# The opening of a transformer block by token halves, and another order of a tile's products

## The chip, the cores and the metric

The kernel runs on one core of a Trainium2 chip. The metric is the device time of one execution in microseconds (us), the smaller the better. The engines have these names in the rows: PE is TensorE (matrix products), PEld its weight loads, DVE is VectorE, ACT is ScalarE, POOL is GpSimd, and SP is the engine that issues most of the transfers from memory (rows of its queue say SPq).

## What is computed

One block for 512 tokens of width 1024 in float32: two token mixers (stick-breaking attention and retention) fed from one wide projection, gates, an output projection, a gated feed-forward layer of width 2816, and norms that are modulated by a condition `c`. The change touches the head of it, the first norm with its modulation, and the first eighth of the projection:

```python
c_act = jax.nn.silu(c)
mod = jnp.einsum('bd,de->be', c_act, w_ada[l]) + b_ada[l]
shift1, scale1, gate1, shift2, scale2, gate2 = jnp.split(mod, N_MOD, axis=-1)
hmix = modulate(rmsnorm(x, g_norm1[l]), shift1, scale1)
proj = jnp.einsum('bsd,de->bse', hmix, w_in[l])
sb_q, sb_k, sb_v, r_q, r_k, r_v, r_g, br = jnp.split(proj, IN_SPLITS, axis=-1)
```

`rmsnorm` divides a token by the root of the mean of its squares over the 1024 features and multiplies by a gain; `modulate(h, shift, scale)` is `h * (1 + scale) + shift`.

## The kernel before

**Layout.** Activations lie with the features on the 128 partitions and the 512 tokens along the free axis. The input x is thus eight tiles `xts[0]` to `xts[7]` (tag `o`) of 128 x 512. `HALVES` are the token columns 0 to 255 and 256 to 511.

**Precision by parts.** A product of float32 precision is made of three faster ones: a tensor is split into a high part (`hi`, made by ScalarE as a rounded copy) and a low part (`lo`, the difference, made by VectorE), and hi x hi, hi x lo and lo x hi are added up in PSUM. Only tile 0 of the opening is multiplied unsplit, as plain float32.

**Loads.** All transfers of the opening go out on SP's queue, in the order of the program text: the small vectors `sm`, the eight tiles of x, a piece of the constants `con`, and then for tile after tile two blocks `sraw` of the modulation matrix (`ada_load`) and one block `raw` of `w_in` (`start_weight`; 256 columns of queries, 256 of keys and 512 of values of the first retention head). A buffer that is still in use makes SP wait, and all that is behind it in its queue. For `raw` there are three buffers, and the low part of the weights, `w_lo`, is one of the instructions that free them.

**Up to the first product.** `ccol` is silu(c). Eight products broadcast it over the partitions (`cb`), and two copies bring it to `cact`. Filler products (`keep_busy`) follow. The squares of the x tiles are made by ScalarE (tile 3 by VectorE); VectorE adds up five of them, and TensorE sums the columns by products with ones, four for each half of the tokens (`ssq`). `dot(n, half)` is a modulation column as a VectorE product with a running sum, `dot_pe(0)` the same by TensorE for the shift of tile 0. `rsqrt_rows` turns a half's sums into `r1` in two ScalarE and three VectorE instructions (lines 327 to 331). `mod_gain` and `mod_shift` (ScalarE, lines 415 and 410) add biases to the columns. `h_t` (VectorE, line 431) multiplies x by gain and `r1`; for tile 0 an addition of the shift follows (ScalarE, line 500).

**The loop over eight tiles** (`kt`, lines 514 to 561) issues the loads of tile kt + 2, the dots of tile kt + 1, the low activations `h_lo` of tile kt (VectorE, line 440), the products of tile kt, then for tile kt + 1 `mod_shift`, `mod_gain`, `w_lo` (VectorE, line 425), `h_t` and the high activations `h_hi` (ScalarE, line 437), and `w_hi` of tile kt + 2 (ScalarE, line 421). Products are 4 of queries and keys (`qk_products`) and 4 of values (`v_products`) for each pair of parts, 24 in all, into eight PSUM banks.

**What sets the order.** TensorE, VectorE and ScalarE run the opening in the order of the program text (`manual_schedule`), each engine strictly through its own queue. Behind the opening a scheduler chooses the order.

Of the kernel before, what the change touches and what calls it, by code (L numbers as in the profile page):

```python
# [11 lines left out]
F32 = mybir.dt.float32  # L12
# [7 lines left out]
P = 128  # L20
# [95 lines left out]
def kernel(  # L116
# [60 lines left out]
    xts = []  # L177
    for j in range(KT):
        xt = otile()
        nc.sync.dma_start(xt, xT[j * P : (j + 1) * P, :])  # L180
        xts.append(xt)
# [4 lines left out]
    nc.sync.dma_start(con[:, P:], consts[:, P:NCON])  # L186
# [198 lines left out]
    for kt in range(2):  # L385
        raws[kt] = ada_load(kt)
        wts[kt] = start_weight(kt)
# [56 lines left out]
    with tc.manual_schedule(engines={nc.vector.engine, nc.scalar.engine, nc.tensor.engine}):  # L444

        nc.scalar.preload_act_table_set("natural_log_exp_and_others")
        c = sm[:, SM_C : SM_C + KT]
# [12 lines left out]
        busy = ps()  # L460

        def keep_busy(n, busy=busy):


            for _ in range(n):
                mm(busy, negones, negones[:, 0:1].to_broadcast([P, S]), True, True)

        keep_busy(8)

        sq = {}  # L470
        for j in range(KT):
            sq[j] = tmp()
            if j == 3:
                nc.vector.tensor_mul(sq[j], xts[j], xts[j])
            else:
                nc.scalar.activation(sq[j], xts[j], AF.Square)
            if j == 4:
                nc.vector.tensor_copy(cact[:, 0:S], cb[0])
            elif j == 6:
                nc.scalar.activation(cact[:, S:], cb[1], AF.Copy)  # L480
            if 0 < j < 5:
                nc.vector.tensor_add(sq[0], sq[0], sq[j])
        ssq = []
        for hv in HALVES:
            o = psz()[:, 0:256]
            for j in (5, 0, 6, 7):
                mm(o, ones, sq[j][:, hv], j == 5, j == 7)
            ssq.append(o)
# [10 lines left out]
        for hv in HALVES:  # L499
            nc.scalar.activation(ts[0][:, hv], ts[0][:, hv], AF.Identity, bias=mods[0, 0])  # L500
        hs.append(pair("h"))
        w_hi(1)
        qk_ps = [ps() for _ in range(3)] + [psa()]
# [10 lines left out]
        for kt in range(KT):  # L514
# [45 lines left out]
            if nx + 1 < KT:  # L560
                w_hi(nx + 1)
# [1264 lines left out]
```

## Time and profile before

| | us |
|---|---|
| three timed executions | 1117.97, 1121.2, 1122.1 |
| their median | 1121.2 |
| the profiled execution | 1119.87 |
| its span, from the first to the last instruction | 1118.2 |
| TensorE busy in it | 1102.5 |
| VectorE busy | 872.0 |
| ScalarE busy | 560.8 |
| first product of tile 0 starts | 16.06 |
| first product of tile 1 starts | 22.62 |

A row of the timeline gives the start and the length in us, the engine, the line, the operation, the tiles it writes and reads, how many instructions are merged in the row, and in brackets how long the engine was idle before it and what ended that. A row of the chain of waits gives a start, a length and what the end of the program, followed back, was held up by. Matrix products overlap in the records, so the spacing of their starts is their price, not their length; a plain float32 product shows as two records. A row of the windows gives a stretch, the busy time of PE, PEld, DVE, ACT and POOL with the number of instructions, then the granted clock, the share of the DMA engines and GB/s. A row of the DMA list gives the transfer, its count, the size of each and the median time from issue to landing.

### The profile page before, as it was taken

The numbers are of one execution on the slowest core, as the hardware profiler recorded it, in microseconds if no ns is written. First come the engines' busy times: TensorE is split into PE (matmuls) and PEld (weight loads), VectorE is DVE, ScalarE is ACT, GpSimd is POOL, SyncE is SP. The second block draws the span as 40 slices with busy tenths as digits, with TensorE's granted clock in tenths as the row PEclk, the third lists the DMA queues.
The fourth block names the chain that finished last, engine by engine and source line by source line (L and its number), as shares of the span: only waits on it lengthen the run. The fifth ranks groups of instructions, "written<-read, shape, count | busy, mean of one in ns | idle before, by whom it ended". The sixth has DMA issues, their size and how long they took to land.

```text
span 1118.2 us, 15055 instructions
## 1 busy us (share of the span) xinstructions
PE 1102.5 (99%) x5607; PEld 937.8 (84%) x5607; DVE 872.0 (78%) x1297; ACT 560.8 (50%) x926; POOL 40.4 (4%) x69
## 2 busy tenths in 40 slices
PE   8999999999999999999999999999999999999996
PEld 7888888888888888888888888789988888888886
DVE  7898866847858768487788767767999889888866
ACT  5455445445434645355655653357745544554443
POOL 0000000010020020000000000000000000000000
PEclk9999999999999999999999999999999999999998
DMA  9825551582484285877676459762443544444112
GB/s 360 300 76 194 196 190 61 178 201 73 169 178 162 89 211 192 212 218 207 177 209 166 152 178 309 244 186 58 123 142 114 151 132 132 129 117 131 58 38 76
DMA packets 60553, 181.42 MB, mean 162 GB/s; under 512 B 7488, under 2 KB 9536, under 8 KB 60480
## 3 DMA queue, kind: packets, MB, share of 16 engines
q1 hardware_dynamic: 54464, 166.30, 45.7%
q0 software_dynamic: 5472, 13.63, 7.8%
q8 instruction: 44, 0.72, 0.3%
q10 hardware_dynamic: 544, 0.52, 0.1%
q14 instruction: 29, 0.24, 0.1%
HBM read 148.97 MB, written 16.78 MB: 148 GB/s over the span
## 4 chain that ended last, share of the span: by engine, by line
PE 90%; DVE 4%; DMA 3%; ACT 2%; issue 1%; SPq 0%; DVEq 0%; ACTq 0%
PE ps L230 65%; PE z L230 14%; PE av L230 8%; DMA araw<-wada 1%; PE ps L642 1%; DMA raw<-wp 1%; DVE araw L261 0%; PE z L770 0%; DMA gspill<-g 0%; DVE wlo L210 0%; PE av L642 0%; DMA t<-spill 0%; ACT q L1205 0%; DVE o L1700 0%; DVE h L1515 0%
## 5 line engine op out<-in xcount | busy, mean ns | idle before, releaser
L230 PE MATMUL ps<-h,whi 128*128 128x512 f32 (+1 forms) x1026 | 295.8, 373 | 2.1 <-ACT h L208 1.3
L230 PEld LDWEIGHTS ps<-h,whi 128*128 128x128 f32 x1026 | 186.0, 189 | 35.6 <-ACT h L208 1.7
L208 ACT ACTIVATE whi<-raw 128x1024 fp32r<-128x1024 f32 (+1 forms) x104 | 108.8, 1046 | 184.6 <-PE ps L230 133.8
L230 PE MATMUL ps<-h,wlo 128*128 128x512 f32 (+1 forms) x513 | 188.6, 371 | 0.0
L210 DVE TENSOR_TENSOR wlo<-raw,whi 128x1024 fp32r<-128x1024 f32 (+1 forms) x104 | 124.9, 1201 | 58.5 <-ACT whi L208 57.8
L230 PEld LDWEIGHTS ps<-h,wlo 128*128 128x128 f32 x513 | 97.1, 189 | 16.7
L230 PE MATMUL ps<-s,whi 128*128 128x512 f32 x320 | 98.9, 390 | 0.0
L230 PE MATMUL ps<-q,whi 128*128 128x512 f32 (+1 forms) x368 | 98.5, 385 | 0.0
L859 DVE TENSOR_TENSOR wlo<-s,whi 128x1024 fp32r<-128x1024 f32 x46 | 56.2, 1222 | 43.8 <-ACT whi L855 43.8
L230 PEld LDWEIGHTS ps<-q,whi 128*128 128x128 f32 x368 | 68.0, 188 | 13.3
L855 ACT ACTIVATE whi<-s 128x1024 fp32r<-128x1024 f32 x47 | 49.7, 1057 | 48.0 <-PE ps L230 39.0
L230 PE MATMUL ps<-whi,h 128*128 128x512 f32 x222 | 71.6, 391 | 0.0
L230 PEld LDWEIGHTS ps<-s,whi 128*128 128x128 f32 x320 | 60.1, 188 | 12.7 <-DVE s L210 0.3
L230 PE MATMUL ps<-s,wlo 128*128 128x512 f32 x160 | 62.2, 389 | 0.0
L230 PE MATMUL ps<-q,wlo 128*128 128x256 f32 (+1 forms) x328 | 59.3, 293 | 0.0
L230 PEld LDWEIGHTS ps<-q,wlo 128*128 128x128 f32 x328 | 48.2, 190 | 3.3
L230 PEld LDWEIGHTS ps<-whi,h 128*128 128x128 f32 x222 | 41.7, 188 | 9.6 <-ACT t L1004 0.6
L230 PE MATMUL ps<-wlo,h 128*128 128x512 f32 x111 | 43.2, 390 | 0.0
L632 DVE TENSOR_TENSOR_SCAN s<-s,table 128x1024 f32<-128x1024 f32 x16 | 36.6, 2288 | 6.7 <-ACT s L626 6.7
L230 PE MATMUL ps<-whi,q 128*128 128x512 f32 x128 | 40.7, 389 | 0.0
L230 PE MATMUL z<-q,q 128*128 128x256 f32 (+3 forms) x224 | 40.1, 325 | 0.0
L230 PEld LDWEIGHTS z<-q,q 128*128 128x128 f32 x224 | 34.8, 189 | 3.0 <-DVE q L210 0.2
(352 smaller groups left out, 2185.9 us busy)
## 6 DMA issues: line engine op xcount, KB each, us to landing
raw<-wp SPq DMA_DIRECT2D x136, 512.0 KB, 3.9
araw<-wp SPq DMA_DIRECT2D x30, 512.0 KB, 4.4
s<-wp SPq DMA_DIRECT2D x24, 512.0 KB, 5.9
araw<-wada SPq DMA_DIRECT2D x18, 512.0 KB, 4.7
sraw<-wada SPq DMA_DIRECT2D x16, 512.0 KB, 8.6
q<-qp SPq DMA_DIRECT2D x32, 256.0 KB, 3.9
s<-wada SPq DMA_DIRECT2D x14, 512.0 KB, 6.8
spill<-o POOLq DMA_DIRECT2D x24, 256.0 KB, 4.3
```

Of the source, the lines that this page charges most:

```text
L208: nc.scalar.activation(dst_hi, src, AF.Copy, scale=scale)
L210: return (eng or nc.vector).tensor_sub(dst_lo, src, f(dst_hi))
L230: return nc.tensor.matmul(o, lhs, rhs, start=start, stop=stop, skip_group_check=True).ins
L632: nc.vector.tensor_tensor_scan(n[:, ::-1], n[:, ::-1], d[:, ::-1], 0.0, op0=ALU.mult, op1=ALU.max)
L642: nc.tensor.transpose(at[bank][:, c : c + P], t[:, a + j * P : a + (j + 1) * P], ident)
L855: nc.scalar.activation(hi, t, AF.Copy)
L859: last_low[0] = nc.vector.tensor_sub(lo, t, f(hi))
```

## The change

The loads are halved and reordered, the norm of the first tokens is separated from that of the second, the fillers are moved, and inside the loop two orders are changed.

```diff
-    xts = []
-    for j in range(KT):
-        xt = otile()
-        nc.sync.dma_start(xt, xT[j * P : (j + 1) * P, :])
-        xts.append(xt)
+    xts = [otile() for _ in range(KT)]
+
+    def load_x(js, hv, queue):
+        for j in js:
+            queue.dma_start(xts[j][:, hv], xT[j * P : (j + 1) * P, hv])
...
-    nc.sync.dma_start(con[:, P:], consts[:, P:NCON])
...
-    for kt in range(2):
-        raws[kt] = ada_load(kt)
-        wts[kt] = start_weight(kt)
+    odd = nc.sync
+    for j in range(KT):
+        load_x((j,), slice(0, 256), odd if j % 2 else nc.sync)
+    raws[0] = ada_load(0)
+    first = wpool.tile([P, WCOLS], F32, tag="raw", bufs=BUFS["raw"], name=nm("raw"))
+    load_x(range(8), slice(256, 512), nc.sync)
+    nc.sync.dma_start(first, wp[WIDX["start", 0]])
+    wts[0] = (first, None, None)
+    raws[1] = ada_load(1)
+    wts[1] = start_weight(1)
+    nc.sync.dma_start(con[:, P:], consts[:, P:NCON])
...
+        busy = ps()
...
+        keep_busy(6)
...
-        keep_busy(8)
-
-        sq = {}
+        def square(j, hv, eng):
+            sq = tmp()[:, 0:256]
...
+        r1 = tmp()
+        h0, h1 = HALVES
+        sums = []
         for j in range(KT):
-            sq[j] = tmp()
+            sq = square(j, h0, nc.vector if j % 2 else nc.scalar)
+            if j in (1, 3, 5):
+                nc.vector.tensor_add(sums[-1], sums[-1], sq)
+            else:
+                sums.append(sq)
             if j == 3:
-                nc.vector.tensor_mul(sq[j], xts[j], xts[j])
-            else:
-                nc.scalar.activation(sq[j], xts[j], AF.Square)
...
+                sq = sums.pop()
+                nc.vector.tensor_add(sums[-1], sums[-1], sq)
+        nc.vector.tensor_copy(cact[:, 0:S], cb[0])
+        nc.scalar.activation(cact[:, S:], cb[1], AF.Copy)
+        s0, s1 = (psz()[:, 0:256] for _ in range(2))
+        column_sums(s0, sums, True, True)
         dot(0, 1)
-        r1 = tmp()
+        keep_busy(4)
         dot_pe(0)
-        keep_busy(3)
-        rsqrt_rows(ssq[0], r1[:, HALVES[0]])
+        rsqrt_rows(s0, r1[:, h0])
         mod_gain(0)
-        h_t(0, HALVES[0])
-        rsqrt_rows(ssq[1], r1[:, HALVES[1]])
-        h_t(0, HALVES[1])
+        h_t(0, h0)
+        column_sums(s1, [square(j, h1, nc.scalar) for j in range(3)], True, False)
         mod_shift(0)
-        for hv in HALVES:
-            nc.scalar.activation(ts[0][:, hv], ts[0][:, hv], AF.Identity, bias=mods[0, 0])
+        identity(h0)
+        three, five = (square(j, h1, nc.vector) for j in (3, 5))
+        nc.vector.tensor_add(three, three, five)
+        seven_ = square(7, h1, nc.vector)
+        keep_busy(4)
+        four, six = (square(j, h1, nc.scalar) for j in (4, 6))
+        nc.vector.tensor_add(three, three, four)
+        nc.vector.tensor_add(six, six, seven_)
+        column_sums(s1, [three, six], False, True)
+        rsqrt_rows(s1, r1[:, h1])
+        h_t(0, h1)
+        identity(h1)
...
                 qk_products(hi, ah, ALL)
+                v_products(ah, hi, range(4))
                 qk_products(lo, ah, ALL)
-                if nx + 1 in PE_SHIFT:
-                    dot_pe(nx + 1)
-                v_products(ah, hi, range(4))
                 v_products(ah, lo, range(4))
...
-                w_lo(nx)
                 h_t(nx)
                 h_hi(nx)
+                w_lo(nx)
```

`odd` is SP's queue too, so all sixteen half tiles go out on the one queue, with the two modulation blocks of tile 0 between the eight first and the eight second halves. `column_sums` multiplies each given tile by ones into one bank; `identity` is the addition of the shift to a half of tile 0.

TensorE ahead of the first product before the change (z_165 and z_170 are the column sums of the two halves, ps_134 takes the fillers, ps_178 is the dot on TensorE, and ps_212 is the first bank of products):

```order
L230 MATMUL ps_134<-negones 128x512 x8
L230 MATMUL z_165<-t_158,ones 128x256
L230 MATMUL z_165<-t_143,ones 128x256
L230 MATMUL z_165<-t_160,ones 128x256
L230 MATMUL z_165<-t_163,ones 128x256
L230 MATMUL z_170<-t_158,ones 128x256
L230 MATMUL z_170<-t_143,ones 128x256
L230 MATMUL z_170<-t_160,ones 128x256
L230 MATMUL z_170<-t_163,ones 128x256
L230 MATMUL ps_178<-mod,sraw_102 128x1 x8
L230 MATMUL ps_134<-negones 128x512 x3
L230 MATMUL ps_212<-o_73,raw_104 128x256
```

The same place now, from the last column sum of the first half on (z_170 is the first half's bank, z_171 the second's, ps_241 the first bank of products):

```order
L230 MATMUL z_170<-t_166,ones 128x256
L230 MATMUL ps_125<-negones 128x512 x4
L230 MATMUL ps_182<-mod,sraw_101 128x1 x8
L230 MATMUL z_171<-t_200,ones 128x256
L230 MATMUL z_171<-t_202,ones 128x256
L230 MATMUL z_171<-t_204,ones 128x256
L230 MATMUL ps_125<-negones 128x512 x4
L230 MATMUL z_171<-t_212,ones 128x256
L230 MATMUL z_171<-t_225,ones 128x256
L230 MATMUL ps_241<-o_73,raw_103 128x256
```

The column sums of the second half, five products in place of four, have moved behind the dot and between two groups of fillers; all of them stand ahead of the first product. Six fillers now stand ahead of the broadcast of c.

VectorE from the second half's scaling of tile 0 to the first low activations, before (o_73 is tile 0, o_75 tile 1; L394 is a dot, L425 the low weights, L431 the scaling):

```order
L431 SCALAR_TENSOR_TENSOR o_73<-o_73,sm_196,t_177 128x256
L394 SCALAR_TENSOR_TENSOR sraw_108,sm_228<-sraw_108,cact 128x1024
L394 SCALAR_TENSOR_TENSOR sraw_110,sm_242<-sraw_110,cact 128x1024
L425 TENSOR_TENSOR wlo_115<-raw_112,whi_114 128x1024
L431 SCALAR_TENSOR_TENSOR o_75<-o_75,sm_245,t_177 128x512
L394 SCALAR_TENSOR_TENSOR sraw_220,sm_260<-sraw_220,cact 128x1024
L440 SCALAR_TENSOR_TENSOR h_249<-o_75,shifts,h_249 128x512
```

And now, from the last sums of the second half on (o_73 is tile 0, o_74 tile 1; the lines have moved by 8: L402 is a dot, L433 the low weights, L439 the scaling; L523 and L524 add squares):

```order
L523 TENSOR_TENSOR t_212<-t_212,t_223 128x256
L524 TENSOR_TENSOR t_225<-t_225,t_217 128x256
L329 SCALAR_TENSOR_TENSOR t_231<-t_231 128x256
L330 SCALAR_TENSOR_TENSOR t_231<-z_171,t_231 128x256
L331 SCALAR_TENSOR_TENSOR t_147<-t_231 128x256
L439 SCALAR_TENSOR_TENSOR o_73<-o_73,sm_197,t_147 128x256
L402 SCALAR_TENSOR_TENSOR sraw_113,sm_257<-sraw_113,cact 128x1024
L402 SCALAR_TENSOR_TENSOR sraw_115,sm_271<-sraw_115,cact 128x1024
L439 SCALAR_TENSOR_TENSOR o_74<-o_74,sm_274,t_147 128x512
L433 TENSOR_TENSOR wlo_120<-raw_117,whi_119 128x1024
L402 SCALAR_TENSOR_TENSOR sraw_249,sm_289<-sraw_249,cact 128x1024
L448 SCALAR_TENSOR_TENSOR h_277<-o_74,shifts,h_277 128x512
```

The scaling of tile 1 now follows directly on the second dot, whose result, by way of the gain on ScalarE, it needs; the low weights have moved behind it. The same holds for every later tile.

More of the change, by code (lines that the diff above doesn't have):

```diff
@@ L483, with column_sums @@
-        ssq = []
-        for hv in HALVES:
[L485 to L488, printed above, removed]
+        def square(j, hv, eng):
+            sq = tmp()[:, 0:256]
+            if eng is nc.vector:
+                nc.vector.tensor_mul(sq, xts[j][:, hv], xts[j][:, hv])
+            else:
+                nc.scalar.activation(sq, xts[j][:, hv], AF.Square)
+            return sq
+        def column_sums(o, sums, first, last):
+            for n, sq in enumerate(sums):
+                mm(o, ones, sq, first and n == 0, last and n == len(sums) - 1)
```

17 lines of the change are left out of this document (6 added, 11 removed).

## The prediction

> **What bounds the kernel now.** I read the page first: the shares of busy time and the shares of the chain of waits.
>
> ```profile
> PE 1102.5 (99%) x5607; PEld 937.8 (84%) x5607; DVE 872.0 (78%) x1297; ACT 560.8 (50%) x926; POOL 40.4 (4%) x69
> PE 90%; DVE 4%; DMA 3%; ACT 2%; issue 1%; SPq 0%; DVEq 0%; ACTq 0%
> ```
>
> TensorE is busy for 1102.5 of 1118.2 us. The change neither removes nor adds a product of the real work, so it can only move the point at which TensorE becomes continuously fed. That point lies in the opening, so I read next the chain of waits over the first 70 us (start, length, what).
>
> ```profile
> 9.93 1.84 PE z L230 x8
> 11.80 0.48 ACT t L327
> 14.20 0.48 DVE o L431
> 14.69 0.35 DVE t L329
> 15.50 0.52 ACT o L500
> 16.06 1.56 PE ps L230 x6
> ```
>
> The column sums of the first half end just before 11.80, the logarithm at L327 starts the norm, L431 scales the first half of tile 0 until 14.68, L500 adds the shift until 16.02, and at 16.06 the first real product starts. Everything ahead of 16.06 is what the change rearranges. Behind it the timeline shows who is short (start, length, engine, line, tiles, idle before).
>
> ```profile
> 22.28 1.22 DVE L394 SCALAR_TENSOR_TENSOR sraw<-sraw,cact 128x1024 f32<-128x1024 f32 x1
> 22.62 0.19 PEld L230 LDWEIGHTS ps<-h,whi 128*128 128x128 f32 x1 [0.24 <-ACT shifts L410]
> 23.42 1.22 DVE L425 TENSOR_TENSOR wlo<-raw,whi 128x1024 fp32r<-128x1024 f32 x1
> 23.54 0.39 ACT L415 ACTIVATE sm<-sm,mod,sm 128x1 f32<-128x1 f32 x1 [1.01 <-DVE sraw L394]
> 24.56 0.74 DVE L431 SCALAR_TENSOR_TENSOR o<-o,sm,t 128x512 f32<-128x512 f32 x1
> 25.34 0.72 ACT L437 ACTIVATE h<-o,shifts 128x512 fp32r<-128x512 f32 x1 [1.41 <-DVE o L431]
> 26.37 0.74 DVE L440 SCALAR_TENSOR_TENSOR h<-o,shifts,h 128x512 fp32r<-128x512 f32 x1
> 33.75 0.64 PEld L230 LDWEIGHTS ps<-h,whi 128*128 128x128 f32 x3
> 39.19 0.64 PEld L230 LDWEIGHTS ps<-h,whi 128*128 128x128 f32 x3
> ```
>
> Tile 1's products start at 22.62. A tile of 24 products then lasts 5.44 us (33.75 to 39.19 is one tile), 0.227 a product. VectorE needs for a tile, start to start: 1.14 for a dot (22.28 to 23.42), 1.14 for the low weights (23.42 to 24.56), 0.66 for the scaling L431, 1.15 for the other dot, and for L440 the rest of a period of 4.75 (L440 of tile 1 starts at 21.61, of tile 2 at 26.37). It runs without a gap, so it is 0.69 a tile faster than TensorE. The last place where TensorE waits for that lead is in the first attention scores:
>
> ```profile
> 21.61 0.75 DVE L440 SCALAR_TENSOR_TENSOR h<-o,shifts,h 128x512 fp32r<-128x512 f32 x1
> 50.53 0.69 DVE L552 TENSOR_TENSOR h<-o,h 128x512 fp32r<-128x512 f32 x1
> 55.93 1.06 ACT L208 ACTIVATE whi<-raw 128x1024 fp32r<-128x1024 f32 x1 [4.38 <-PE z L230]
> 57.02 1.23 DVE L210 TENSOR_TENSOR wlo<-raw,whi 128x1024 fp32r<-128x1024 f32 x1 [4.21 <-ACT whi L208]
> 70.75 0.69 DVE L210 TENSOR_TENSOR q<-t,q 128x512 fp32r<-128x512 f32 x1
> 71.49 1.29 PEld L230 LDWEIGHTS z<-q,q 128*128 128x128 f32 x10 [0.24 <-DVE q L210]
> ```
>
> VectorE idles 4.21 us before 57.02 and then has no gap up to the low part q that ends at 71.44; TensorE idles 0.24 for it. At this join whichever of the two is later decides; after it I count a shift as carried to the end.
>
> **The change, part by part.** The sum is made on the profiled execution: 1118.2 us of span, 1119.87 in all. The three timed runs have a median of 1121.2 (1117.97 to 1122.1); with the profiled one the median of four is 1120.5, and that is what I put my shift on.
>
> *Loads.* The prices of the loads and of the early work:
>
> ```profile
> 1.25 3.74 SPq L180 DMA_DIRECT2D o<-xT  x8
> 7.60 1.99 ACT L476 ACTIVATE t<-o 128x512 f32<-128x512 f32 x3 [0.71 <-DMA o<-xT]
> 11.15 1.23 DVE L394 SCALAR_TENSOR_TENSOR sraw<-sraw,cact 128x1024 f32<-128x1024 f32 x1 [1.00 <-DMA sraw<-wada]
> 17.46 1.06 ACT L421 ACTIVATE whi<-raw 128x1024 fp32r<-128x1024 f32 x1 [0.45 <-DMA raw<-wp]
> 9.50:13.30 3.80, 3.80 (x18) 3.17 (x18) 2.39 (x6) 2.26 (x6) 0.00 (x0) 1.00 1.02 407
> o<-xT SPq DMA_DIRECT2D x8, 256.0 KB, 4.3
> raw<-wp SPq DMA_DIRECT2D x136, 512.0 KB, 3.9
> out_dram<-o SPq DMA_DIRECT2D x8, 128.0 KB, 1.8
> ```
>
> SP issues a tile load every 0.47 us. Sixteen halves instead of eight wholes add eight issues, 3.8 us of SP: the last second half goes out near 9.8, the first weight near 10.2 instead of 6.93, the second near 11.6 instead of 8.95. This hides behind the queue, which moves 407 GB/s (last figure of the stretch 9.5 to 13.3), 1.29 us per 512 KB, and is behind anyway: the first modulation half lands at 11.15, so the first weight lands at 13.7 and the second at 17.5 (seen at 17.46). Ahead of the first weight stand the same bytes as before, so 13.7 stays. If the rows of half length moved more slowly, the cover would be gone by what they lose. The first halves are 1 MB; before, 1.25 MB were there at 7.60, so I take 6.9 for the last first half. The nearest transfer of that size, a store at the end of the kernel, lands 1.8 after its issue; from the last issue at 4.5 that gives 6.3, and a store need not price a load, so 6.3 to 7.6.
>
> *TensorE up to the first product.*
>
> ```profile
> 1.10 0.23 DVE L198 TENSOR_SCALAR negones<-ones 128x128 fp32r<-128x128 f32 x1
> 3.50:5.40 1.90, 1.86 (x9) 1.89 (x10) 0.00 (x0) 0.91 (x2) 0.00 (x0) 1.00 0.97 314
> 3.54 3.75 PE L230 MATMUL z<-con,mod 128*128 128x128 f32 x16 [3.54 <-DVE mod L456]
> 6.95 2.98 PE L230 MATMUL ps<-negones 128*128 128x512 f32 x8
> 9.77 3.72 PE L230 MATMUL z<-t,ones 128*128 128x256 f32 x16
> 13.32 1.84 PE L230 MATMUL ps<-mod,sraw 128*128 128x1 f32 x16
> 77.32 1.42 DVE L915 TENSOR_TENSOR s<-o 128x256 f32<-128x256 f32 x4
> ```
>
> Six filler products, which can start at 1.33, cost 6 x 0.37 = 2.2 and end near 3.6; the broadcast of c follows for 3.75, until 7.3, as before (7.29), so the filler at the front costs nothing on the path. Eight column sums took 3.72, 0.465 each; the four of the first half need the last square (6.9 + 0.36 on VectorE = 7.3) and end at 7.3 + 1.9 = 9.2 instead of 11.7. Broadcast products of 128 columns cost as much as column sums of 256, so TensorE was at half pace early on, though the granted clock reads 1.00 in that stretch (third figure from the end, 3.5 to 5.4). The eight fillers from 6.95 average 0.37, between 0.45 and 0.227: five slow and three fast, so the pace doubled near 9.2. If it stays slow until then again, the sums end at 10.0; if it speeds up while c is broadcast, at 8.6. I take 9.2, since TensorE now starts 2.2 us sooner. The Trainium skill (TensorE: Matmul & The Clock Gate, "What's actually happening") has full rate after a busy window of about 3.4 us that runs freely; worked out from 1.4 that would be an estimate of 4.8 to 8.2 and would put the sums at 8.6 to 9.2, while this trace left half pace only about 5.7 us after TensorE's first product at 3.54.
>
> Behind these sums TensorE's own queue now holds, before the first product: four fillers (0.9 at 0.227), the dot on TensorE (1.84), three column sums (1.4), four fillers (0.9), two column sums (0.9): 6.0 in all. The other path has the same length: the norm from L327 to the end of L431 took 2.88, then six VectorE operations on halves at 0.36 (L915: 1.42 for four) and their waits, 2.4, then one sum, 0.5. So the first product starts at 9.2 + 6.0 = 15.2 (14.6 to 16.0), not at 13.7, where the weight would allow it: the second half's sums stand ahead of it in the same queue. Gain so far 0.9 of 16.06.
>
> *Tile 1.* Now the second half's norm runs under the first half's products (3.5 us, 16.06 to 19.6 before). From the product's start: 0.1 to L327, 2.8 until VectorE is free behind the second L431 (11.80 to 14.69 in the first, less the 0.1 that the next waited), two dots 2.28, the wait for the gain, L431 0.74, L437 0.72 and 0.04 between. The wait is new: the low weights stood between the dot and the scaling and covered it. The dot ends at 23.42, the gain at 23.93, so 0.55 lies bare; nothing else is queued on VectorE that could fill it. Sum 7.2: tile 1 starts at 22.4 instead of 22.62. TensorE would be ready at 15.2 + 6.56 = 21.8, so 0.6 of the 0.9 is given back here.
>
> *Value products of high parts first, low weights after the scaling.* These two go together: low weights are needed eight products into a tile (1.8 us) instead of four, and end 1.2 behind the scaling. That costs TensorE nothing. The tile on VectorE becomes 4.75 + 0.55 = 5.30, still 0.14 under 5.44, so there is no stall from tile 2 on, but the lead no longer grows by 0.69 a tile. The loads that wait for low weights go out later; a weight load lands in 3.9 us (median of the 136), and its buffer is wanted again two tiles, 10.6 us, after such a release, so that stays hidden; without that cover tile 4 would wait.
>
> *The join.* Scaling of tile 1 starts at 20.9 and of tile 7 six periods later at 52.7; then scaling, low weights, low activations, tile 0's low part and the first stored weight's low part (L431 0.66, 1.14, L440 0.67, L552 0.6, 1.14) bring VectorE to 56.9 instead of 57.02. Its 4.21 us of idle time are used up. TensorE is 0.2 earlier and had 0.24 of idle, so VectorE decides: the end moves by about -0.1 us, bounds -0.7 (sums at 8.6) to +0.9 (sums at 10.0 and a wait of 0.6).
>
> **The rivals.**
>
> 1. *Forecast: the earlier start is given back*, -0.1 us, 1120.4. Chance 0.62.
>
> 2. *Faster: more of it is kept.* If the first halves are summed by 8.3, the product starts at 14.3, tile 1 at 21.5 and the join 0.9 sooner; the limit is the weight at 13.7, which gives 1.5. Time 1119.0 to 1119.6. For it: the loads' eight tiles were square-limited late (three back to back from 7.60). Against it: the 6 us of TensorE's queue follow the sums whatever they do. Chance 0.16.
>
> 3. *Slower: VectorE becomes the bound of every tile.* Its place is the wait for the gain; it decides from 0.69 on, where the period passes 5.44. If ScalarE reaches the gain 0.5 late, because it is still at the high weights (1.06), the period is 5.80, tile 7 starts 2.2 late and the join 6 x 0.5 = 3.0 late. Time 1123.4. For it: the lead is gone and ScalarE's order is fixed. Against it: ScalarE idled 1.01 before that gain and has 2.2 us of work in a tile (0.72, 1.06 and 0.39) and a small addition. Chance 0.12.
>
> 4. *Slower: halves are loaded at the price of wholes.* If every half took SP's and the queue's pace for a whole, 0.64, the second halves need 5.1 us instead of 2.6, the first weight lands at 16.2, the last square of the second half is made near 15.3 and the product starts near 16.6; tile 1 at 23.8, +1.2, and 1121.7. For it: a load's landing took 4.3 in the median and the queue was slow at first. Against it: SP had issued all wholes by 5, long before they landed, so bytes and not issues set the pace. Chance 0.07. The Trainium skill (DMA: Bandwidth & Descriptors, "Bandwidth") asks for 1 MiB or more in a transfer; its table, for another queue, gives an estimate of 1.3 us for a half and 2.0 for a whole, 4.9 more for sixteen in a row, and no row here shows loads in a row like that.
>
> The other 0.03 is for what I have not seen, such as TensorE falling back to half pace between the fillers.
>
> **How the numbers follow.** What a measurement of this kernel tells from no change is about 0.5%, 5.6 us. All cases lie between -1.5 and +3, so nearly all the chance is on no change: 0.95; faster by over 0.5% 0.02, slower 0.03 for a wait that grows beyond rival 3. The time is 1120.5 - 0.1 = 1120.4. Executions of the unchanged kernel spread from 1117.97 to 1122.1, more than the cases do, so the range is that spread with the cases' bounds: 1117.5 to 1123.4.
>
> **What would show it.** The logarithm at L327 near 9.3 instead of 11.80; the first product near 15.2 with the last two column sums right before it; a new idle of about 0.55 on VectorE before each scaling of 512 columns, put down to the gain; tile 1 near 22.4 after an idle of about 0.6 on TensorE; the second stored weight's low part near 57 without the idle of 4.21; the join near 71.4. A first product before 14.5, or a period of VectorE over 5.44, would say that rival 2 or 3 holds. The prediction is wrong if the time moves by over 5 us, which only something outside the first 72 us could do.

## The result, and the profile after

| | before | after |
|---|---|---|
| executions beside each other | 11 | 11 |
| median, us | 1119.35 (1116.63 to 1122.94) | 1124.39 (1122.02 to 1126.51) |
| profiled execution: span | 1118.2 | 1122.9 |
| first product of tile 0 | 16.06 | 18.92 |
| first product of tile 1 | 22.62 | 26.24 |
| the join in the attention scores | 71.49 | 75.06 |

The ratio is 1.0043, with a 95% interval of 1.003 to 1.0056. The kernel became about 5 us slower; 1124.39 lies above the predicted 1117.5 to 1123.4. In the profiled execution 3.6 us of it are there at the join. A further 1.2 us appear at a pause of TensorE near 725 us, whose first wait lasts 1.3 us in before and 2.5 in after. Over the 13 profiled executions of this document that wait lasts 1.3 to 1.9 us in seven and 2.3 to 2.6 in six, and those six are after and five edits of it (the long filler, the old loop order, whole loads with the long filler, the fillers at the old place and the wide dot). A half pace follows the pause in all six, and of the seven in before alone. With one profile of each kernel it is not shown whether the change lengthens the pause.

The timeline of after in the opening (start, length, engine, line, operation, tiles, and in brackets the idle before it and what ended that):

```profile
9.27 0.47 ACT L327 ACTIVATE t<-z,eps 128x256 f32<-128x256 f32 x1 [1.29 <-PE z L230]
10.70 1.22 DVE L402 SCALAR_TENSOR_TENSOR sraw<-sraw,cact 128x1024 f32<-128x1024 f32 x1 [1.67 <-DMA sraw<-wada]
12.32 1.95 PE L230 MATMUL ps<-mod,sraw 128*128 128x1 f32 x16 [2.22 <-DMA sraw<-wada]
14.13 2.58 PE L230 MATMUL z<-t,ones 128*128 128x256 f32 x6
14.60 0.51 ACT L491 ACTIVATE o<-o,sm 128x256 f32<-128x256 f32 x1
16.15 2.07 PE L230 MATMUL ps<-negones 128*128 128x512 f32 x4
18.06 1.03 PE L230 MATMUL z<-t,ones 128*128 128x256 f32 x4
18.92 1.46 PE L230 MATMUL ps<-o,raw 128*128 128x256 f32 x6
22.54 1.16 PEld L230 LDWEIGHTS ps<-o,raw 128*128 128x128 f32 x6 [0.84 <-ACT o L491]
24.68 0.75 DVE L439 SCALAR_TENSOR_TENSOR o<-o,sm,t 128x512 f32<-128x512 f32 x1 [0.45 <-ACT sm L423]
26.24 0.54 PEld L230 LDWEIGHTS ps<-h,whi 128*128 128x128 f32 x3 [0.82 <-ACT h L445]
```

The change does the first half of what it says: the first half's norm begins at 9.27 instead of 11.80, and the first half of tile 0 is scaled and shifted at 15.11 (the fifth row's end) instead of 16.02. But TensorE's queue is not ready for it. Its dot of single columns waits until 12.32 for the second modulation half, and behind it stand three column sums, four fillers and two column sums, so that the product begins 3.8 us after its half of the tokens was ready.

The same stretch in windows of about 3.4 us (stretch, its length, busy time and count of PE, PEld, DVE, ACT and POOL, granted clock, share of the DMA engines, GB/s):

```profile
7.60:11.10 3.50, 2.43 (x10) 1.79 (x10) 1.44 (x4) 1.27 (x3) 0.00 (x0) 1.00 0.95 309
11.10:14.50 3.40, 2.18 (x18) 2.15 (x19) 2.93 (x7) 1.75 (x5) 0.00 (x0) 1.00 0.90 296
14.50:17.90 3.40, 3.40 (x10) 2.69 (x9) 1.95 (x5) 1.34 (x4) 0.00 (x0) 0.50 0.97 361
17.90:21.30 3.40, 3.40 (x16) 2.80 (x15) 1.15 (x3) 0.89 (x2) 0.00 (x0) 1.00 1.03 401
```

From 14.5 to 17.9 the granted clock is 0.50. That explains why six records of column sums last 2.58 us and four fillers 2.07; the run with the long filler shows both at full pace, 1.54 and 1.22. The chain of waits (start, length, what) names what led there (rows of issue, 0.04 us and less, left out):

```profile
5.04 0.43 SPq L374
5.52 6.76 DMA sraw<-wada
12.32 1.95 PE ps L230 x16
14.27 2.44 PE z L230 x6
16.71 1.51 PE ps L230 x4
18.22 0.86 PE z L230 x4
19.09 1.29 PE ps L230 x6
```

The rows of SP's queue show what became of the loads:

```profile
1.26 3.74 SPq L181 DMA_DIRECT2D o<-xT  x8
6.01 6.62 SPq L181 DMA_DIRECT2D o<-xT  x8
12.67 0.43 SPq L391 DMA_DIRECT2D raw<-wp  x1
```

and its waits (engine and line, what ended them, total us, times, longest):

```profile
SPq L181 <- DMA sraw<-wada: 2.6, 2, 1.4
```

The first eight halves are issued in 3.74 us as forecast, the second eight take 6.62, of which 2.6 is waiting for the two modulation loads to land. Thus the first weight goes out at 12.67, not at 10.2; the list of transfers gives this load 4.3 us from issue to landing, so it landed near 17.0, not at 13.7. With halves the queue moved about 300 GB/s from 7.6 to 14.5, against 407 before (9.5 to 13.3).

### The profile page after: what moved, and what is told of

The parts are those of the page before. It is cut to its first block, busy times and chain, and to the rows that moved or that the text cites. A ratio compares the mean times of both kernels' runs of the same rounds, so it can differ in the third digit from the quotient of the medians.

```text
span 1122.9 us, 15091 instructions
## 1 busy us (share of the span) xinstructions
PE 1105.2 (98%) x5612; PEld 938.5 (84%) x5612; DVE 874.5 (78%) x1306; ACT 561.5 (50%) x928; POOL 40.6 (4%) x69
## 4 chain that ended last, share of the span: by engine, by line
PE 90%; DVE 4%; DMA 3%; ACT 1%; issue 1%; SPq 0%; DVEq 0%; ACTq 0%
PE ps L230 66%; PE z L230 14%; PE av L230 8%; PE ps L669 1%; DMA raw<-wp 1%; DMA araw<-wada 1%; DMA sraw<-wada 1%; DVE wlo L210 1%; DVE araw L261 0%; DMA gspill<-g 0%; PE z L797 0%; PE av L669 0%; SPq L181 0%; ACT q L1232 0%; DVE o L1727 0%
## 5 line engine op out<-in xcount | busy, mean ns | idle before, releaser
L230 PEld LDWEIGHTS ps<-h,wlo 128*128 128x128 f32 x513 | 97.0, 189 | 16.6
L230 PEld LDWEIGHTS ps<-q,whi 128*128 128x128 f32 x368 | 68.0, 188 | 13.3
```

The source lines that it names most:

```text
L230: return nc.tensor.matmul(o, lhs, rhs, start=start, stop=stop, skip_group_check=True).ins
```

## The experiments

Letters in the expectations: O is the orders inside the loop, L the loads, G the granted clock, Q the order of TensorE's queue. Each was timed beside executions of before on the same chip. In the table the clock is the mean granted clock of the timed executions. Some 0.003 of its distance from 1 costs no time: behind the last product TensorE has nothing to do, and the clock is at 0.50 until the end (in after from 1117.0 to 1122.9), so that the profiles whose records hold no other half pace read 0.997. "Half" counts the windows of 3.4 us at half pace that the profiled execution shows before tile 1.

| kernel | ratio (95%) | clock | half | product | tile 1 | join |
|---|---|---|---|---|---|---|
| before | | 0.9960 | 0 | 16.06 | 22.62 | 71.49 |
| after | 1.0043 (1.003 to 1.0056) | 0.9936 | 1 | 18.92 | 26.24 | 75.06 |
| loop order alone | 1.0001 (0.999 to 1.0013) | 0.9957 | 1 | 16.28 | 24.55 | 73.38 |
| whole-tile loads | 1.0036 (1.0024 to 1.0048) | 0.9945 | 1 | 19.05 | 26.37 | 75.17 |
| long filler | 1.0007 (0.9993 to 1.0022) | 0.9963 | 0 | 17.26 | 24.53 | 73.33 |
| old loop order | 1.003 (1.0017 to 1.0043) | 0.9948 | 1 | 18.89 | 26.81 | 75.37 |
| whole loads, long filler | 1.0037 (1.0022 to 1.0053) | 0.9953 | 0 | 18.41 | 25.74 | 74.56 |
| all sums before the dot | 1.0017 (1.0003 to 1.003) | 0.9958 | 0 | 17.91 | 24.50 | 73.34 |
| fillers at the old place | 1.0029 (1.0015 to 1.0043) | 0.9947 | 2 | 20.82 | 28.14 | 76.95 |
| wide dot | 1.003 (1.0016 to 1.0045) | 0.9948 | 0 | 17.69 | 25.01 | 73.83 |
| old opening, wide dot | 0.9991 (0.9977 to 1.0004) | 0.9965 | 0 | 15.96 | 22.55 | 71.40 |
| products before sums | 1.0036 (1.0021 to 1.0051) | 0.9955 | 1 | 17.45 | 28.75 | 77.58 |
| fewer sums, constants last | 1.0003 (0.999 to 1.0017) | 0.9963 | 0 | 15.65 | 22.24 | 71.09 |

**Loop order alone.** The kernel before with the two orders of the loop (products, and low weights behind the scaling), nothing else.

```diff
                 qk_products(hi, ah, ALL)
+                v_products(ah, hi, range(4))
                 qk_products(lo, ah, ALL)
-                if nx + 1 in PE_SHIFT:
-                    dot_pe(nx + 1)
-                v_products(ah, hi, range(4))
...
-                w_lo(nx)
                 h_t(nx)
                 h_hi(nx)
+                w_lo(nx)
```

`PE_SHIFT` holds tile 0 alone, so the two lines on it never ran in the loop.

> The kernel before with the two orders inside the loop alone (value products of high parts second, low weights behind the scaling), loads and norm as before. Theory L (halved loads bring the modulation block and the first weight late) and theory G (TensorE falls to half pace in the gap before its dot) both put the loss ahead of the first product: they expect the first product at 16.1, tile 1 at 22.6 and no change of time (within 1 us). Theory O (the new order in the loop costs the time, because the wait for the gain lies bare on VectorE) expects tile 1 near 22.6 but the join at the first scores 2 to 4 us later and the time 2 to 4 us longer.

The ratio is 1.0001 (0.999 to 1.0013), so the loop's orders carry none of the loss that could be told, and theory O, which gave 2 to 4 us, falls. Its profile brought a surprise, in the windows:

```profile
13.40:16.80 3.40, 3.27 (x23) 2.78 (x22) 3.13 (x8) 1.75 (x5) 0.00 (x0) 1.00 1.03 412
16.80:20.20 3.40, 3.40 (x8) 2.36 (x7) 2.95 (x6) 2.04 (x4) 0.00 (x0) 0.50 1.02 407
```

Here the old opening, too, has a window at half pace, 16.8 to 20.2, and tile 1 is 1.9 late in this execution although its first product is only 0.2 late. So the half pace is not the change's own: the question is how often an execution has it.

**Whole-tile loads.** After, with x in eight whole tiles ahead of tile 0's modulation; the other loads keep after's order.

```diff
-    odd = nc.sync
     for j in range(KT):
-        load_x((j,), slice(0, 256), odd if j % 2 else nc.sync)
+        load_x((j,), slice(0, 512), nc.sync)
     raws[0] = ada_load(0)
...
-    load_x(range(8), slice(256, 512), nc.sync)
     nc.sync.dma_start(first, wp[WIDX["start", 0]])
```

> The changed kernel with x loaded in eight whole tiles again, in the order x, modulation of tile 0, first weight, and so on; norm and sums stay by halves. Theory L expects the first sums near 10.2 (one us later than with halves), TensorE's dot at 12.2, the first weight at 13.7 instead of about 17, the first product near 17.3 instead of 18.9, tile 1 near 24.6, and 1.5 us less than the changed kernel. Theory Q (the queue order of TensorE, not the loads, sets the first product) expects the same 17.3 but no less than that, since the second half's sums and two groups of fillers follow the dot in either case. Theory O expects no change from the changed kernel.

The timeline of this kernel, SP's row first:

```profile
6.52 0.33 SPq L389 DMA_DIRECT2D raw<-wp  x1
12.45 1.95 PE L230 MATMUL ps<-mod,sraw 128*128 128x1 f32 x16 [0.47 <-DMA sraw<-wada]
15.89 2.27 PE L230 MATMUL ps<-negones 128*128 128x512 f32 x4
19.05 1.46 PE L230 MATMUL ps<-o,raw 128*128 128x256 f32 x6
```

and its windows:

```profile
11.60:15.00 3.40, 2.93 (x22) 2.47 (x21) 3.21 (x8) 2.29 (x8) 0.00 (x0) 1.00 1.04 414
15.00:18.40 3.40, 3.40 (x10) 2.64 (x9) 1.48 (x5) 0.96 (x3) 0.00 (x0) 0.50 1.03 396
```

The weight is issued 6 us earlier than in after, and the product comes no earlier. Modulation lands when it did, the dot starts at 12.45, and the half pace is there, although TensorE's gap ahead of the dot is only 0.47 us. The slow halves and the late weight are real, but they are not what holds the product.

**Long filler.** After, with more fillers in front of the dot.

```diff
         dot(0, 1)
-        keep_busy(4)
+        keep_busy(14)
         dot_pe(0)
```

> The changed kernel with 14 instead of 4 filler products behind the first sums, so that TensorE does not idle for 2.2 us ahead of its dot. Theory G expects full pace from 12.3 on: three sums, four fillers and two sums in 3.2 us instead of 4.8, the first product near 17.4 instead of 18.9 and 1.5 us less time. Theory L alone expects the first product no earlier than the first weight lands, about 17. If the pace has nothing to do with the gap, the first product stays at 18.9.

```profile
9.01 3.41 PE L230 MATMUL ps<-negones 128*128 128x512 f32 x14
12.28 1.95 PE L230 MATMUL ps<-mod,sraw 128*128 128x1 f32 x16
14.09 1.54 PE L230 MATMUL z<-t,ones 128*128 128x256 f32 x6
15.28 1.22 PE L230 MATMUL ps<-negones 128*128 128x512 f32 x4
17.26 1.53 PE L230 MATMUL ps<-o,raw 128*128 128x256 f32 x6
```

This timeline has no half pace: the same six records of column sums take 1.54 instead of 2.58, the fillers 1.22 instead of 2.07, and the product starts 1.66 earlier than in after. Ten idle products more take the ratio from 1.0043 to 1.0007, and the clock of the executions from 0.9936 to 0.9963. Theory G is borne out, and by more than the 1.5 us that it gave: by the ratios some 4 us. What remains here, 1.2 us at the product and 1.8 at the join, is not a half pace in the opening. The first weight, issued at 12.63 and 4.5 us on its way, lands near 17.1, just ahead of the product at 17.26: with the clock kept, the late weight comes next.

**Old loop order.** After, with the loop as before (the reverse of the first diff).

> The changed kernel with the order inside the loop as before (low products of queries and keys second, low weights ahead of the scaling). Theories L and G expect the first product unchanged at 18.9. For tile 1 the low weights take 1.14 between the dot and the scaling where the bare wait was 0.5, so I expect tile 1 at 26.8 instead of 26.2, 0.6 us more time. Theory O expects 2 to 3 us less time than the changed kernel.

Tile 1 starts at 26.81, 0.57 later than in after, since the low weights again stand ahead of the scaling; the ratio of 1.003 cannot be told from after's 1.0043. In the opening of after the new order is worth about half a microsecond at tile 1, and its worth at the end is not resolved.

**Whole loads and long filler.** Both edits at once.

> The kernel after with both single edits at once: x loaded in eight whole tiles as before, the first weight ahead of the second modulation block and the constants last, and 14 fillers in place of 4 behind the first sums. Theory G+Q (half pace and TensorE's own queue; the loads hardly matter because the queue behind the second modulation half sets the first product): full pace in the opening, dot of columns near 12.4, first product 17.3 to 17.5 although the first weight lands four microseconds earlier than with the halves, tile 1 near 24.6, ratio to before 1.0005 to 1.002, as with the long filler alone (1.0007). Theory L (the late first weight holds the product at 17): product near 16.3, tile 1 near 23.6, ratio 0.9995 to 1.0005.

A miss. With whole tiles the first sums end later, and 14 fillers from 10.35 then pushed the dot to 13.60 and the product to 18.41. No half pace in the profile, ratio 1.0037. It tells nothing of the loads, but shows the price of a filler that is too long: the dot came 1.2 us late, and the product did too.

**All sums before the dot.** Whole tiles, the second half squared and summed tile by tile ahead of the first half's norm. TensorE gets eight fillers ahead of the dot and three behind it; the lines on that and on the buffers are left out here.

```diff
...
+            sq = square(j, h1, nc.vector if j in (1, 3) else nc.scalar, both[:, h1])
+            mm(s1, ones, sq, j == 0, j == KT - 1)
...
-        column_sums(s1, [square(j, h1, nc.scalar) for j in range(3)], True, False)
...
-        column_sums(s1, [three, six], False, True)
-        rsqrt_rows(s1, r1[:, h1])
...
```

> Whole tiles as in the run before, but the second half of the tokens is squared and summed as each tile lands, in front of the first half's norm, so that TensorE's queue holds only fillers between its dot and the first product and the second half's chain no longer runs behind the first's. Theory Q (order of the queue, and the second half's chain in series): dot of columns at 12.4, first product at 15.3 (scale and shift of the first half end at 15.1 in the kernel after), second half's products without a wait, tile 1 at 21.9 to 22.2 against 22.6 before, ratio to before 0.9985 to 1.0000. Rival (halves of the tokens cost by themselves, whatever the order, with their double count of short instructions on ScalarE and VectorE): squares end so late that the first sums come at 12 and the product at 16.5 or later, tile 1 at 23.1 or later, ratio 1.0005 or more.

```profile
9.44 4.15 PE L230 MATMUL z<-t,ones 128*128 128x256 f32 x18 [0.98 <-DVE t L478]
13.24 2.10 PE L230 MATMUL ps<-negones 128*128 128x512 f32 x8
13.69 0.47 ACT L327 ACTIVATE t<-z,eps 128x256 f32<-128x256 f32 x1 [2.41 <-PE z L230]
17.91 1.56 PE L230 MATMUL ps<-o,raw 128*128 128x256 f32 x6
```

The rival was nearer: 16 squares of half length and 12 column sums fill the time, the first half's sums come last in TensorE's queue and end at 13.6, and the advantage of the halves is gone. But the second half's products now start at 21.45, 3.54 behind the first's, without a wait, and the step from product to tile 1 is 6.6, as in before, instead of 7.3.

**Fillers at the old place.** After, without the six fillers at the front, with the eight of before behind the broadcast of c.

```diff
-        keep_busy(6)
         c = sm[:, SM_C : SM_C + KT]
...
+        keep_busy(8)
+
         def square(j, hv, eng):
```

> The kernel after with its six fillers at the front taken out and the eight of before put back behind the broadcast of c. Theory G (the gap of 2 us and the dot of single columns behind it bring the half pace): the clock opens near 9 instead of 4.2, and half pace still comes in part of the executions; first product at 17.3 to 18.9, time 1122.5 to 1124.5. Rival W (the clock opened too early by the fillers at the front): no half pace in the opening, product near 17.3, time 1121 to 1122, as with the long filler.

Rival W falls: the half pace came in two windows in a row, 13.5 to 20.3, and the ratio is 1.0029. The fillers at the front are not what brings it.

**Wide dot.** After, with the dot done for 64 equal columns.

```diff
-            mm(o[:, 0:1], raws[n][0][:, k * P : (k + 1) * P], ccol[:, k : k + 1],
+            mm(o[:, 0:64], raws[n][0][:, k * P : (k + 1) * P], ccol[:, k : k + 1].to_broadcast([P, 64]),
                k == 0, k == KT - 1)
```

> The kernel after, with TensorE's dot of columns done for 64 equal columns instead of one (the same 16 weight loads, column 0 is used as before), and the short fillers and the gap of 2 us ahead of it left as they are. Theory G1 (the granted clock goes by how much TensorE did in the 3.4 us ahead: the dot of single columns counts as idle beside the gap): with 64 columns the 3.4 us hold enough, no half pace in the opening, first product 17.3, mean granted clock of the runs 0.996 as in before, time 1121 to 1122, ratio 1.0007 to 1.002. Rival G2 (the gap alone does it, whatever the dot does): half pace as before the edit, first product 18.9, mean clock 0.994, time 1123.5 to 1124.5.

Between the two theories. In the profiled execution the opening keeps its pace (product at 17.69), but the mean clock rises only to 0.9948, half way back, and 1122.99 us is above what G1 gave. The dot of 64 columns takes 2.00 instead of 1.95, so it is free. The window that holds it:

```profile
11.90:15.30 3.40, 2.67 (x20) 2.60 (x21) 3.14 (x8) 2.05 (x6) 0.00 (x0) 1.00 0.78 224
```

Beside the dot there are 0.67 us of other work in it, less than in some windows with the single columns behind which the clock fell, and the next window ran at 1.00. The gap of 2 us ahead of the dot is left, and seems enough in part of the executions; that is not shown.

**Old opening, wide dot.** The kernel of the first experiment with the wide dot.

> The kernel before with the two loop orders of the change and the dot of columns for 64 equal columns: opening by whole tokens, loads as before. If half pace in the opening of the kernel before (seen in the run with the loop order alone, 16.8 to 20.2) also comes from the dot of single columns, the mean granted clock rises from 0.9957 to 0.9965 or more and the time falls to 1118.5 to 1119.5, ratio 0.9985 to 0.9995: below both kernels. Rival (those executions come from elsewhere, such as the pause near 723 us): clock 0.9957 to 0.9961, ratio 0.9995 to 1.0010.

The clock rises from 0.9957 to 0.9965, and the median is 1118.72 against 1119.93 of before beside it. The interval, 0.9977 to 1.0004, includes no change, so this is the lowest ratio here and not a kernel shown to be faster.

**Products before sums.** Whole tiles, wide dot, five fillers, and tile 0's first-half products ahead of the second half's sums (the diff shows the order alone).

```diff
...
+        qk_products(raw, ts[0], h0, True)
+        column_sums(s1, firsts, True, False)
         column_sums(s1, [three, six], False, True)
+        v_products(ts[0], raw, (0, 1), True)
         rsqrt_rows(s1, r1[:, h1])
         h_t(0, h1)
         identity(h1)
...
```

> Whole tiles with the first weight early, wide dot, five fillers behind the first sums and none later, and the first half's products of tile 0 ahead of the second half's column sums in TensorE's queue (the query-key ones ahead of the sums, the value ones behind). Theory Q+S (the queue holds the first product, and the second half's chain of squares, sums, norm, gain and shift in series behind the first's holds tile 1): first product at 15.2 to 15.6 in place of 17.3, but second half's sums end near 17.7, its products start at 21.0 to 21.5 after a wait of 1.5 us or more, tile 1 at 24.7 to 25.2: three microseconds gained at the first product are not passed on, ratio 1.0010 to 1.0025. Rival (the first product alone sets tile 1, 6.6 to 7.3 behind it): tile 1 at 21.9 to 22.7, ratio 0.9985 to 1.0000.

```profile
6.90:10.30 3.40, 0.96 (x6) 0.59 (x5) 1.70 (x5) 0.83 (x2) 0.00 (x0) 1.00 1.02 380
10.30:13.70 3.40, 3.32 (x9) 2.46 (x8) 2.61 (x5) 0.93 (x3) 0.00 (x0) 0.50 1.03 419
```

These windows show that TensorE had little to do until 10.3 and was at half pace until 13.7, so the dot came at 14.66 and the product at 17.45, not at 15.2. The timeline shows the rest:

```profile
17.45 1.56 PE L230 MATMUL ps<-o,raw 128*128 128x256 f32 x6 [0.89 <-ACT o L489]
21.64 0.47 ACT L327 ACTIVATE t<-z,eps 128x256 f32<-128x256 f32 x1 [2.58 <-PE z L230]
25.05 1.56 PE L230 MATMUL ps<-o,raw 128*128 128x256 f32 x6 [1.74 <-ACT o L489]
```

The product now starts as soon as its data are there. But the second half's norm begins at 21.64, its products at 25.05 behind a wait of 1.74, and tile 1 at 28.75, 11.3 behind the first product. An early first half is not passed on: the second half's chain, queued behind it, sets tile 1. The rival's 6.6 to 7.3 is excluded.

**Fewer sums, constants last.** The old opening with the wide dot, 12 instead of 16 records of column sums, and the constants behind the weights (the diff shows the sums alone).

```diff
...
-            if 0 < j < 5:
+            if 0 < j < 6:
                 nc.vector.tensor_add(sq[0], sq[0], sq[j])
...
-            for j in (5, 0, 6, 7):
-                mm(o, ones, sq[j][:, hv], j == 5, j == 7)
+            for j in (6, 0, 7):
+                mm(o, ones, sq[j][:, hv], j == 6, j == 7)
```

> The run with the old opening, new loop order and wide dot, with two more edits from what was learned: VectorE adds one more tile's squares, so that TensorE sums 3 tiles a half instead of 4 (12 matmuls of 0.23 us instead of 16), and the constants are loaded last, so that modulation and weight land earlier. The dot of columns stood behind the sums at 13.2. Theory Q (the queue ahead of the first product sets tile 1): dot at 12.3 to 12.6, first product at 15.2 to 15.5 against 15.96, tile 1 at 21.9 to 22.2 against 22.55, time 1118.0 to 1119.0, ratio 0.9975 to 0.9990. Rival (norm, gain and shift on VectorE and ScalarE hold the product): product at 15.8 or later, ratio 0.9985 to 0.9997, the same as without the edits.

Product at 15.65, tile 1 at 22.24, join 0.4 earlier than before: half of the gain that was forecast, and in time nothing (1.0003). No kernel here beats the one before beyond its uncertainty.

## Why the prediction was wrong

Two causes make up most of the loss. Over 244 executions of the 13 kernels of the table, fitted with one level for each kernel and one slope for the clock, an execution takes 1.37 us more for each 0.001 that its mean granted clock is lower. One window of 3.4 us at half pace is 1.7 / 1122 = 0.0015 of clock. After has 0.9936 and before 0.9960: some 1.6 windows more in an execution, 3.3 us by the slope. At equal clock after stands 1.25 us above before, plus or minus 0.6; the long filler, which has after's queue without its half pace, stands at 1.6. The split is not sharp. Pace alone would cost 1.12 us for 0.001 (a thousandth of 1122), so the slope holds other things that go with a low clock; by 1.12 the clock's part is 2.7 us and the rest 1.9. The fit does not tell where in an execution the windows lie, either. The longer pause near 725 does not account for the clock: the long filler's profile has it too (2.3 us), and its executions have the clock of before. The profiles show the opening, for one execution each: after's join is 3.6 late with one such window in the opening, the long filler's 1.8 late without, and the run with the fillers at the old place shows that one opening can have two.

**The failed step: the clock.** The text had TensorE's queue at full pace throughout (0.227 a filler, 0.465 a column sum) and left 0.03 for "what I have not seen, such as TensorE falling back to half pace between the fillers". That is the larger part of the loss, and no term stood for it. The price of half pace was in the prediction's own rows (a filler at 0.45 against 0.227); what was not asked is whether the change makes a thin stretch in TensorE's work. It does: fillers end at 10.1, the dot waits until 12.32, and then runs single columns. In the windows next ahead of each half pace, TensorE's busy time without the dot of single columns is 0.2 us of 3.4 in after (2.18 less 1.95), 0.55 with the old loop order (2.50 less 1.95), about 1.0 with whole-tile loads (2.93 less 1.95), and 1.4 with the loop order alone (3.27 less 1.84) and with the fillers at the old place (2.30 less the 0.94 of the dot that lies in it). With products before sums the window ahead holds no dot and 0.96 us of work. That the single columns count as idle was argued so; the wide dot, with 0.67 us of other work and no half pace behind it, supports it without settling it.

The Trainium skill (TensorE: Matmul & The Clock Gate, "HAM oscillation — how this bites in real kernels") puts the rule as no idle gaps of TensorE over about 3.4 us. By that rule the gap of 2.2 us in after is harmless; this case's trace differs, with half pace behind a gap of 2.2 us and 1.95 us of single columns, and with whole tiles behind a gap of 0.47 us and such a dot, and the measurement decides. The Trainium skill (TensorE: Matmul & The Clock Gate, "What's actually happening") has a window of 3413 ns that runs freely; with this the traces agree, for each half pace in an opening lasted 3.4 us or twice that and stood at 14.5, 16.8, 13.5 or 10.3, not at a fixed place in the program.

**The second failed step: the queue behind the sums, "6.0 in all".** It let the dot start when the four fillers end, at 10.1. The dot needs the second modulation half. The text had the first modulation half landing at 11.15, and in the same sentence the rate of 1.29 us per 512 KB, which puts the second at 12.4; the two were not joined. Measured: 12.32. From there the sum holds: at full pace the long filler's product starts 5.0 behind its dot, where the terms (1.84, 1.4, 0.9 and 0.9) give 5.0. So 15.2 became 17.3 by this step and 18.9 by the clock.

**The loads.** First halves: the norm at 9.27, as forecast (9.3), but in part by luck. The last first half was there near 8.0 (its square on VectorE starts at 8.00, behind a wait for the load), not at 6.9, and outside the 6.3 to 7.6 that were given; the end came right because three sums were left to make from 7.67, where the text had four from 7.3. "13.7 stays" was wrong. The weight was issued at 12.67 instead of 10.2, because SP waits for earlier loads to land and halves move more slowly. Rival 4, which gave a product at 16.6 and 1121.7 us, had that mechanism, but whole tiles with an early weight gained nothing (1.0036), so it is not the cause. The halves' rate, about 300 GB/s against 407, points the same way as the Trainium skill (DMA: Bandwidth & Descriptors, "Bandwidth"), which asks for transfers of 1 MiB and more, on figures for another queue; here that cost lay beside other waits.

**From product to tile 1.** Forecast 7.2, measured 7.3, and the terms hold: 0.2 to the second half's norm, 2.7 until VectorE is free, 2.3 for two dots, then the bare wait for the gain (forecast 0.55, measured 0.45) and the scaling. That VectorE sets tile 1 was right: its weight loads wait 0.82 for the scaled tile, where 0.6 was forecast. The wait of 0.84 ahead of the second half was not forecast, but it is one of the weight loads; the second half's products start 3.62 behind the first's, against 3.55 before.

**Fillers at the front, the loop's orders, the join.** The fillers at the front show no cost: with them the broadcast of c ended at 6.1 instead of 7.3, and the run without them is not told from after (1.0029 and 1.0043, with intervals that overlap). The loop's orders were forecast at nothing but the small shift at the join, and gave 1.0001. Rival 3, VectorE as the bound of every tile, did not occur: the scalings of tiles 1 and 2 start 5.30 apart (24.68 and 29.98), as the sum had it, and 3.6 us at tile 1 are 3.57 at the join. A shift at the join is there at the end to within about 2 us in each profile; what is added or lost goes in the main with the length of the pause near 725 and with a half pace behind it. So the join was right, and the shift that it passed on had the wrong size and sign.

**What was taken for no change.** The text took 0.5% for what a measurement can tell and put 0.95 on no change. The loss is 0.43%, and with 11 executions of each kernel its interval, 1.003 to 1.0056, excludes no change. That a move of over 5 us could only come from outside the first 72 us was wrong too: the move is 5.04 us, and 3.6 us of it were there at the join.

What stays open: how much activity in a window keeps the clock, and how much the single columns count. Beside its dot, before has 1.56 us of work in the window from 12.4 to 15.8 and kept the clock, while 1.6 us in the first half-pace window of the run with the fillers at the old place were followed by another at half pace.

## What to carry to other kernels

When work at the start is moved, list for each engine not only what runs when but where it will be idle or nearly so, and ask of every instruction that is moved up whether its own data come up too: here the norm came 2.5 us earlier, and the modulation behind it less than half a microsecond (the first dot at 10.70 instead of 11.15). TensorE can lose its clock behind a thin stretch, as it did here, so a gap made by an earlier start wants work in it that lasts until the awaited data land, and no longer. Splitting a chain in two helped nothing here, because only the first half's end came earlier: its head start ends where the second half queues behind it.

## What was not expected of the hardware

The half pace comes in the middle of the kernel too. Windows of before at the pause of TensorE near 723 us:

```profile
719.00:722.40 3.40, 3.40 (x17) 2.81 (x16) 2.70 (x4) 0.63 (x1) 0.00 (x0) 1.00 0.94 312
722.40:725.80 3.40, 1.26 (x6) 0.49 (x4) 2.72 (x4) 1.58 (x2) 0.00 (x0) 1.00 0.22 88
725.80:729.20 3.40, 3.40 (x8) 2.75 (x9) 2.20 (x3) 2.47 (x3) 0.00 (x0) 0.50 0.48 159
```

One window with 1.26 us of work is followed by one at clock 0.50. With all sums before the dot, the same pause fell across two windows and no half pace followed in that execution: counted back in steps of 3.41 us from the clock's fall near 1111.9, behind its last product, a window ends at 726.2, and the waits end at 726.56 and 727.90 in the rows below.

```profile
726.56 0.50 PE L230 MATMUL ps<-h,whi 128*128 128x512 f32 x1 [1.43 <-ACT h L208]
727.90 0.50 PE L230 MATMUL ps<-h,whi 128*128 128x512 f32 x1 [0.84 <-DVE h L210]
```

So part of the spread of 1117 to 1124 us between executions of one kernel goes with the granted clock: the 24 executions of before at 0.995 took 1121.4 us on average, the 28 at 0.997 took 1118.6.

With sixteen loads of 128 KB in the queue, two modulation blocks among them, it moved about 300 GB/s (309 and 296 in the windows above); with eight whole tiles of 256 KB and the same blocks it moved 410 from 8.2 to 11.6. SP's two waits in after, 2.6 us together, stand in its program at the seventh and eighth second half, eight loads behind the two modulation loads whose landing ends them: each of these two loads waits for the eighth one ahead of it.
